# The order of the sixteen row blocks in the last FFN-down sweep of a decoder layer: plain squares and pairs of the seven-product form in turn

## The chip, the cores and the metric

The kernel runs on one core of a Trainium2 chip. The metric is the device time of one execution in microseconds (us). TensorE is called PE, VectorE DVE, ScalarE ACT, GpSimd POOL; SP is the engine whose queue issues the transfers. "L1239" is line 1239 of the kernel before; the change adds one line at 1174, so that every later line stands one number higher in the kernel after.

## The reference

One decoder layer over 256 tokens of width 2048 in float32. Only the last third matters here:

```python
x = x + mix @ w_out
h2 = rms_norm(x, mlp_norm)
x = x + jnp.square(jax.nn.relu(h2 @ w_ffn_up)) @ w_ffn_down      # 2048 -> 8192 -> 2048
gate = jax.nn.sigmoid(rms_norm(x, ple_norm) @ w_ple_gate)
x = x + gate * (p @ w_ple_proj)
out = rms_norm(x, final_norm)
```

`mix` is the output of the mixers that come before (pooling and RWKV-7). The change touches the product with `w_ffn_down` alone.

## The kernel before

**Products in two parts.** Each float32 operand is split into a high part (a copy rounded to PE's format, ACT) and a low part (what the rounding lost, DVE). A product is then three matmuls: high by high, low by high, high by low. Every weight therefore crosses ACT once and DVE once before PE can use it: `wh`, `wl` are high and low of a plain weight block, `w7h`, `w7l` of the blocks that the seven-product form uses as they are, `th`, `tl` of the sums of blocks that it needs.

**The FFN.** The 8192 hidden columns are worked in two halves (`hf` 0 and 1). In each half the up product gives 16 blocks of squared activations of 256 hidden columns each (numbers 0 to 15), and two down sweeps follow, one for each half of the 2048 output columns (`np_`). The tiles of a sweep carry both numbers: `d00`, `d01`, `d11`, `d10` in order of time. `d10` is the last one; it gives output columns 0 to 1023.

**A sweep** (`sweep`, L1311) goes through the 16 blocks in the order of a table (`ORDER[j_]`, `j_` being 0 for the first and 1 for the second sweep of a half). A block is a 2x2 product of squares: 256 hidden columns and 256 tokens on one side, 256 hidden columns and 1024 output columns on the other. Ten blocks (`SEVEN`) are done with seven products of 128x512 tiles instead of eight, 21 matmuls, at the price of sums of weight blocks; the other six (`PLAIN`: 2, 5, 8, 11, 14, 15) are plain squares of 24 matmuls, two splits on DVE and no sums. For six of the ten in the second sweep (0, 3, 4, 7, 10, 12, from `AHEAD`) the sums were made earlier and are read back from memory (`tr`, or two `raw` buffers for the blocks in `BY_RING`); blocks 1, 6, 9, 13 make theirs in the sweep: four extra DVE operations on `raw` (L1293 to L1296).

Within a block of the seven-product form there are four products with sums (`of_sums`: `t1`, `t3`, `t2`, `t4`, high parts first, then low) and three with plain blocks (`of_blocks`). Sums come first after a plain square, blocks first after another block of the seven-product form:

```python
for part in (of_sums, of_blocks) if seq[pos - 1] in PLAIN else (of_blocks, of_sums):
    part()
```

so two neighbours run as sums, blocks, blocks, sums. A third one in a row runs again as blocks, sums.

**Buffers.** `th` and `tl` exist once: the sums of the next block are converted only when PE has read the last ones. Raw weights have a ring of seven buffers, high parts of five, low parts of four, given out in the order of use, so a low part can be written only after the one four places earlier has been read. Eight PSUM banks hold the sweep's results: `p2`, `p3`, `p4`, `d22` (one bank each, fed by both kinds of block) and `p5`, `p7`, `p1`, `p6` (two double banks `w1`, `w2`, fed by the seven-product form alone).

**The end of a sweep.** After the last block of the seven-product form (13 in either order) ACT copies `p1` (L1389), DVE combines `p6`, `p7`, `p5` with it (`u`, L1390 to L1392) and adds the result into the residual stream `xb` for both token halves (two operations of 128x1024, L1411). After the last block of all, the four other banks are added one by one (`residual_` on `p2`, `p3`, `p4`, `d22`, 128x512 each, L1411). In the last sweep the first of these frees the bank into which the next stage's first product goes: `pp`, the projection of the per-layer embeddings (L1475 onward; its first bank is the one of `p2`, its second that of `p3`), whose 48 matmuls alternate with transposes of the new `xb` (`h3t`, L1157) and are followed by the gate product `gt`. The fourth quarter of the gate's weights (`gk`) is split ahead and kept.

**What sets the order.** A scheduler places the instructions of this part by priorities and by its own estimate of when operands are ready: splits, sums and residuals carry high priorities, and each engine then runs its list strictly in order. Three hooks hang on positions in the sweep, not on block numbers: at 12 one half of the residual stream is loaded (`xb` from `xd`, into the slot of block 4's activations), at 13 the other half (into the slot of `tr`), at 15 the embeddings `p` are loaded and split (`ps`).

## Time and profile before

| | us |
|---|---|
| median of 3 runs (lowest, highest) | 1163.5 (1162.97, 1163.73) |
| the profiled execution: its own time | 1163.34 |
| the profiled execution: span from first to last instruction | 1161.6 |
| busy: PE, PE's weight loads, DVE, ACT | 1150.8, 989.2, 920.6, 689.1 |

The time of an execution stands 1.74 us above its span, which begins with the first instruction and ends with the last. A row of the timeline gives the start, the busy time from the first start to the last end of the merged instructions, the engine, the line, the operation, output and inputs, and the count; matmuls overlap in the records, so PE's pace is read from one start to the next. "[x <-Y]" at a row's end is idle time before it and what ended it. SPq is the queue of transfers.

### The profile page before, as it was taken

What the parts mean: (1) busy time and instruction counts of PE and PEld (TensorE: products, weight loads), DVE (VectorE), ACT (ScalarE), POOL (GpSimd) and SP (SyncE); (2) the same over time, 40 slices, a digit from 0 to 9 for tenths busy, and PEclk for the clock granted to TensorE, in tenths of its full rate; (3) what the DMA queues carried; (4) which work ended last, traced back from release to release, by engine and by line L of the source; (5) the groups of instructions that cost most, each with busy time, mean ns of one, the idle gap of its engine ahead of it and who ended that gap; (6) DMA issues with size and microseconds to landing.
All of it is one profiled execution on the core that took longest, in us unless ns stands there. A gap on an engine that the chain in (4) does not pass through costs nothing.

```text
span 1161.6 us, 19313 instructions
## 1 busy us (share of the span) xinstructions
PE 1150.8 (99%) x7348; PEld 989.2 (85%) x7348; DVE 920.6 (79%) x1223; ACT 689.1 (59%) x1220; POOL 17.2 (1%) x77
## 2 busy tenths in 40 slices
PE   9999999999999999999999999999999999999997
PEld 8999998788888888888888888888888888888886
DVE  7886898356676788888989888888878989888843
ACT  5868555667544655555665755555556665669733
POOL 4100000000000000000000000000000000000000
PEclk9999999999999999999999999999999999999999
DMA  7553544453898999985787887998885778996812
GB/s 274 164 171 127 160 151 152 147 165 109 319 328 277 325 342 343 326 327 191 257 291 250 319 298 280 350 332 328 317 302 180 262 266 287 335 327 227 301 36 73
DMA packets 78445, 290.87 MB, mean 250 GB/s; under 512 B 8720, under 2 KB 9744, under 8 KB 74128
## 3 DMA queue, kind: packets, MB, share of 16 engines
q1 hardware_dynamic: 78064, 289.28, 70.8%
q8 instruction: 57, 0.93, 0.3%
q10 hardware_dynamic: 288, 0.37, 0.1%
q14 instruction: 36, 0.29, 0.1%
HBM read 259.20 MB, written 30.41 MB: 249 GB/s over the span
## 4 chain that ended last, share of the span: by engine, by line
PE 96%; DVE 1%; DMA 1%; ACT 1%; issue 0%; DVEq 0%; ACTq 0%; SPq 0%
PE u_w L1135 21%; PE d_p L1239 15%; PE u_w L1140 10%; PE d_w L1239 9%; PE d_d L1239 3%; PE o_b L193 2%; PE o_b L195 2%; PE o_b L194 2%; PE gt_b L193 2%; PE gt_b L195 2%; PE gt_b L194 2%; PE zp_b L193 2%; PE wag_b L380 1%; PE zr_b L184 1%; PE zk_b L184 1%; PE zk_b L185 1%
## 5 line engine op out<-in xcount | busy, mean ns | idle before, releaser
L1135 PE MATMUL u_w<-h,wh_u 128*128 128x512 f32 x1024 | 321.9, 395 | 0.0
L1140 PEld LDWEIGHTS u_w<-h,wl_u 128*128 128x128 f32 x1024 | 192.4, 188 | 45.4
L171 ACT ACTIVATE wh_u<-raw_u 128x512 fp32r<-128x512 f32 x256 | 147.2, 623 | 133.9 <-PE u_w L1135 99.8
L1140 PE MATMUL u_w<-h,wl_u 128*128 128x256 f32 x1024 | 201.4, 278 | 0.0
L172 DVE TENSOR_TENSOR wl_u<-raw_u,wh_u 128x1024 fp32r<-128x1024 f32 x128 | 156.1, 1220 | 38.1 <-PE u_w L1140 22.6
L1135 PEld LDWEIGHTS u_w<-h,wh_u 128*128 128x128 f32 x1024 | 156.1, 189 | 0.1
L1299 ACT ACTIVATE th_d<-raw_d 128x1024 fp32r<-128x1024 f32 x52 | 52.6, 1053 | 63.1 <-DVE raw_d L1295 43.7
L1239 PE MATMUL d_p<-wh_d,yd 128*128 128x512 f32 x288 | 77.0, 389 | 0.0
L1301 DVE TENSOR_TENSOR tl_d<-raw_d,th_d 128x1024 fp32r<-128x1024 f32 x52 | 61.4, 1221 | 12.4 <-ACT th_d L1299 12.3
L172 DVE TENSOR_TENSOR wl_o<-raw_o,wh_o 128x1024 fp32r<-128x1024 f32 x32 | 39.0, 1223 | 31.3 <-ACT wh_o L171 15.9
L1239 PEld LDWEIGHTS d_p<-wh_d,yd 128*128 128x128 f32 x288 | 54.0, 188 | 11.3
L1239 PE MATMUL d_w<-th_d,ys 128*128 128x512 f32 x240 | 61.5, 390 | 0.0
L171 ACT ACTIVATE wh_o<-raw_o 128x512 fp32r<-128x512 f32 x64 | 36.7, 623 | 40.2 <-PE o_b L194 21.7
L171 ACT ACTIVATE wh_d<-raw_d 128x512 fp32r<-128x512 f32 x96 | 53.9, 619 | 7.0 <-DMA raw_d<-in_w_ffn_down_dram 2.7
L172 DVE TENSOR_TENSOR wl_d<-raw_d,wh_d 128x1024 fp32r<-128x1024 f32 x48 | 57.1, 1217 | 0.0
L1288 ACT ACTIVATE w7h_d<-raw_d 128x1024 fp32r<-128x1024 f32 x40 | 42.2, 1056 | 22.1 <-DMA raw_d<-in_w_ffn_down_dram 8.4
L1239 PEld LDWEIGHTS d_w<-th_d,ys 128*128 128x128 f32 x240 | 44.7, 188 | 9.6 <-ACT th_d L1299 0.5
L1290 DVE TENSOR_TENSOR w7l_d<-raw_d,w7h_d 128x1024 fp32r<-128x1024 f32 x40 | 48.8, 1219 | 4.4 <-PE d_d L1239 2.0
L1239 PE MATMUL d_p<-w7h_d,ys 128*128 128x512 f32 x160 | 49.3, 389 | 0.0
L1239 PE MATMUL d_p<-wl_d,yd 128*128 128x512 f32 x144 | 44.3, 389 | 0.0
L1289 ACT ACTIVATE w7h_d<-raw_d 128x512 fp32r<-128x512 f32 x40 | 25.0, 624 | 24.4 <-PE d_d L1239 19.5
L172 DVE TENSOR_TENSOR wl_zp<-raw_zp,wh_zp 128x1024 fp32r<-128x1024 f32 x16 | 19.5, 1223 | 24.6 <-ACT wh_zp L171 24.6
(390 smaller groups left out, 2694.5 us busy)
## 6 DMA issues: line engine op xcount, KB each, us to landing
raw_u<-in_w_ffn_up_dram SPq DMA_DIRECT2D x128, 512.0 KB, 6.3
raw_d<-in_w_ffn_down_dram SPq DMA_DIRECT2D x106, 512.0 KB, 5.9
raw_ta<-in_w_ffn_down_dram SPq DMA_DIRECT2D x44, 512.0 KB, 6.8
tad<-ta SPq DMA_DIRECT2D x22, 1024.0 KB, 5.7
raw_o<-in_w_out_dram SPq DMA_DIRECT2D x32, 512.0 KB, 5.2
tr_d<-tad SPq DMA_DIRECT2D x28, 512.0 KB, 5.1
raw_gt<-in_w_ple_gate_dram SPq DMA_DIRECT2D x24, 512.0 KB, 4.6
raw_zk<-in_w_in_dram SPq DMA_DIRECT2D x16, 512.0 KB, 3.5
```

The costliest lines, as they stand in the source:

```text
L171: nc.scalar.activation(wh[:, a * 512 : (a + 1) * 512], raw[:, a * 512 : (a + 1) * 512], AF.Copy)
L172: nc.vector.tensor_tensor(wl, raw, wh.bitcast(F32), op=ALU.subtract)
L193: nc.tensor.matmul(o, a_h, wh[:, 0:n], start=first, stop=False)
L194: nc.tensor.matmul(o, a_l, wh[:, 0:n], start=False, stop=False)
L195: nc.tensor.matmul(o, a_h, wl[:, 0:n], start=False, stop=last)
L1135: nc.tensor.matmul(bank[:, ct, :].rearrange("p (s t) -> p s t", s=2), wh[:, c], hl, start=k == 0, stop=False, skip_group_check=True,)
L1140: nc.tensor.matmul(bank[:, ct, 0:T], wl[:, c], hl[:, 0, :], start=False, stop=k == 15, skip_group_check=True)
L1239: nc.tensor.matmul(o, l, r, start=first, stop=last, skip_group_check=True)
L1288: nc.scalar.activation(ha, ra, AF.Copy)
L1290: nc.vector.tensor_tensor(la, ra, ha.bitcast(F32), op=ALU.subtract)
L1299: nc.scalar.activation(th[:, r], tr[r], AF.Copy)
L1301: nc.vector.tensor_tensor(tl[:, r], tr[r], th[:, r].bitcast(F32), op=ALU.subtract)
```

## The change

The last sweep gets an order of its own, the other three keep theirs. Seven-product blocks now always stand in pairs, a plain square between each two pairs, and one plain square (15) at the end instead of two (14, 15).

```diff
     ORDER = (tuple(range(16)), (2, 0, 1, 3, 5, 4, 6, 7, 8, 9, 10, 11, 12, 13, 14, 15))
+    LAST = (2, 0, 1, 5, 3, 4, 8, 6, 7, 11, 9, 10, 14, 12, 13, 15)
     SEVEN = tuple(i for i in range(16) if i not in PLAIN)
...
-        seq = ORDER[j_]
+        seq = LAST if hf and j_ else ORDER[j_]
```

No instruction with arithmetic on PE is added or removed; the sweep's matmuls, splits, sums and transfers are the same ones in another order. Up to the fourth block (2, 0, 1) both orders agree. Three places show how the engines' lists moved. In the names `d10_0_13` is the first, `d10_1_13` the second raw tile of block 13 in the sweep `d10`; `ys6` are the activations of block 6.

**PE, between block 6 and block 7.** Before:

```order
L1239 MATMUL d10_p4_9921<-tl_d10_6_10179,ys6_8247 128x512
L1239 MATMUL d10_w2_9924<-w7h0_d10_7_10226,ys7_8355 128x512 x2
L1239 MATMUL d10_w2_9924<-w7l0_d10_7_10228,ys7_8355 128x512
L1239 MATMUL d10_p2_9919<-w7h1_d10_7_10227,ys7_8355 128x512 x2
L1239 MATMUL d10_p2_9919<-w7l1_d10_7_10229,ys7_8355 128x512
L1239 MATMUL d10_p3_9920<-w7h0_d10_7_10226,ys7_8355 128x512 x2
L1239 MATMUL d10_p3_9920<-w7l0_d10_7_10228,ys7_8355 128x512
L1239 MATMUL d10_w1_9923<-th_d10_7_10224,ys7_8355 128x512 x4
```

After:

```order
L1240 MATMUL d10_p4_9921<-tl_d10_6_10217,ys6_8247 128x512
L1240 MATMUL d10_w2_9924<-w7h0_d10_6_10218,ys6_8247 128x512 x2
L1240 MATMUL d10_w2_9924<-w7l0_d10_6_10220,ys6_8247 128x512
L1240 MATMUL d10_p2_9919<-w7h1_d10_6_10219,ys6_8247 128x512 x2
L1240 MATMUL d10_p2_9919<-w7l1_d10_6_10221,ys6_8247 128x512
L1240 MATMUL d10_p3_9920<-w7h0_d10_6_10218,ys6_8247 128x512 x2
L1240 MATMUL d10_p3_9920<-w7l0_d10_6_10220,ys6_8247 128x512
L1240 MATMUL d10_w2_9924<-w7h0_d10_7_10264,ys7_8355 128x512 x2
```

Before, 6 and 7 followed block 4, 6 began with its blocks, and 7 therefore had only its own nine block matmuls between the sums of 6 and its own sums. After, 6 follows the plain square 8 and begins with its sums, and the blocks of 6 and of 7 lie between the two groups of sums.

**DVE, from the low parts of block 13 to the residual additions.** Before, from the second low part of block 14:

```order
L172 TENSOR_TENSOR wl_d10_1_14_10527<-raw_d10_1_14_10519,wh_d10_1_14_10526 128x1024
L177 TENSOR_TENSOR ps_10561<-raw_pT_10559,ps_10561 128x512
L172 TENSOR_TENSOR wl_d10_0_15_10565<-raw_d10_0_15_10555,wh_d10_0_15_10564 128x1024
L1390 TENSOR_TENSOR u_d10_10510<-d10_w2_9924,u_d10_10510 128x512
L172 TENSOR_TENSOR wl_d10_1_15_10570<-raw_d10_1_15_10557,wh_d10_1_15_10569 128x1024
L1391 TENSOR_TENSOR u_d10_10510<-d10_w1_9923,u_d10_10510 128x512
L1392 TENSOR_TENSOR u_d10_10510<-u_d10_10510,d10_w1_9923 128x2x512
L1411 SCALAR_TENSOR_TENSOR xb4_10469<-u_d10_10510,s2sq_4333,xb4_10469 128x1024 x2
L1411 SCALAR_TENSOR_TENSOR xb4_10469<-d10_p2_9919,s2sq_4333,xb4_10469 128x512
L172 TENSOR_TENSOR wl_pp0_0_10610<-raw_pp0_0_10607,wh_pp0_0_10609 128x1024
L1411 SCALAR_TENSOR_TENSOR xb4_10469<-d10_p3_9920,s2sq_4333,xb4_10469 128x512
```

After, from the low parts of 13's sums:

```order
L1302 TENSOR_TENSOR tl_d10_13_10510<-raw_d10_0_13_10505,th_d10_13_10509 128x1024
L1302 TENSOR_TENSOR tl_d10_13_10510<-raw_d10_1_13_10507,th_d10_13_10509 128x1024
L172 TENSOR_TENSOR wl_d10_0_15_10565<-raw_d10_0_15_10555,wh_d10_0_15_10564 128x1024
L172 TENSOR_TENSOR wl_d10_1_15_10570<-raw_d10_1_15_10557,wh_d10_1_15_10569 128x1024
L172 TENSOR_TENSOR wl_pp0_0_10610<-raw_pp0_0_10607,wh_pp0_0_10609 128x1024
L1391 TENSOR_TENSOR u_d10_10548<-d10_w2_9924,u_d10_10548 128x512
L172 TENSOR_TENSOR wl_pp1_0_10650<-raw_pp1_0_10647,wh_pp1_0_10649 128x1024
L1392 TENSOR_TENSOR u_d10_10548<-d10_w1_9923,u_d10_10548 128x512
L1393 TENSOR_TENSOR u_d10_10548<-u_d10_10548,d10_w1_9923 128x2x512
L177 TENSOR_TENSOR gk01_10809<-raw_gk0_10806,gk00_10808 128x512
L1412 SCALAR_TENSOR_TENSOR xb4_10464<-u_d10_10548,s2sq_4333,xb4_10464 128x1024 x2
L1412 SCALAR_TENSOR_TENSOR xb4_10464<-d10_p2_9919,s2sq_4333,xb4_10464 128x512
```

Before, the four low parts of 14 and 15 come after 13's sums, and the combination `u` and the residuals are run while PE works on 14 and 15. After, only 15 is left behind 13; between 13's sums and the residual of `p2` there now also stand the low parts of the first two tiles of the projection (`wl_pp0`, `wl_pp1`) and one of the kept gate weights (`gk01`), which all stood behind the residual of `p2` before.

**SP's queue, the transfers around the end of the sweep.** Before (the second tile of 13 and the load of `xb4` stand right ahead of the first row):

```order
L163 DMA raw_d10_0_14_10517<-in_w_ffn_down_dram 128x1024
L163 DMA raw_d10_1_14_10519<-in_w_ffn_down_dram 128x1024
L163 DMA raw_d10_0_15_10555<-in_w_ffn_down_dram 128x1024
L163 DMA raw_d10_1_15_10557<-in_w_ffn_down_dram 128x1024
L163 DMA raw_pT_10559<-in_pT_dram 128x512
L1482 DMA fn_10765<-in_final_norm_dram 128x2048
L163 DMA raw_pp0_0_10607<-in_w_ple_proj_dram 128x1024
L163 DMA raw_pp1_0_10647<-in_w_ple_proj_dram 128x1024
L163 DMA raw_pp2_0_10687<-in_w_ple_proj_dram 128x1024
L163 DMA raw_pp3_0_10727<-in_w_ple_proj_dram 128x1024
L163 DMA raw_gt0_0_10787<-in_w_ple_gate_dram 128x1024
L163 DMA raw_gk0_10806<-in_w_ple_gate_dram 128x1024
```

After:

```order
L1483 DMA fn_10765<-in_final_norm_dram 128x2048
L1420 DMA xb4_10464<-xd3_6935 128x2048
L163 DMA raw_d10_1_13_10507<-in_w_ffn_down_dram 128x1024
L163 DMA raw_d10_0_15_10555<-in_w_ffn_down_dram 128x1024
L163 DMA raw_d10_1_15_10557<-in_w_ffn_down_dram 128x1024
L163 DMA raw_pT_10559<-in_pT_dram 128x512
L163 DMA raw_pp0_0_10607<-in_w_ple_proj_dram 128x1024
L163 DMA raw_pp1_0_10647<-in_w_ple_proj_dram 128x1024
L163 DMA raw_gt0_0_10787<-in_w_ple_gate_dram 128x1024
L163 DMA raw_pp2_0_10687<-in_w_ple_proj_dram 128x1024
L163 DMA raw_pp3_0_10727<-in_w_ple_proj_dram 128x1024
L163 DMA raw_gk0_10806<-in_w_ple_gate_dram 128x1024
```

The final norm's weights (`fn`, 1 MB) and `xb4` (1 MB) have moved ahead of the second tile of block 13, and `gt0_0` ahead of the last two tiles of the projection. The load of `gk0` keeps its place behind these.

## The prediction

> **What bounds the kernel now.** I read the page first: busy time and the chain of waits.

> ```profile
> PE 1150.8 (99%) x7348; PEld 989.2 (85%) x7348; DVE 920.6 (79%) x1223; ACT 689.1 (59%) x1220; POOL 17.2 (1%) x77
> PE 96%; DVE 1%; DMA 1%; ACT 1%; issue 0%; DVEq 0%; ACTq 0%; SPq 0%
> ```

> PE is the bound, and the chain that ended last runs on it for 96% of the span. So the change can gain only where PE stands, and loses wherever it makes PE stand. Next the list of PE's waits (line waited for: us in all, times, longest us), and the stages from the last sweep on (stretch: length, then busy us of PE, weight loads, DVE, ACT, POOL; granted clock, DMA share, GB/s):

> ```profile
> PE warm_b L349 <- DVE ones L107: 1.2, 1, 1.2
> PE h2t L1157 <- DVE h L1164: 0.4, 1, 0.4
> PE zp_b L195 <- DVE wl_zp L172: 0.3, 1, 0.3
> 969.90:1050.50 80.60, 80.60 (x355) 66.28 (x354) 72.88 (x79) 48.80 (x69) 0.00 (x0) 1.00 0.90 324
> 1050.50:1064.20 13.70, 13.70 (x74) 11.21 (x72) 12.15 (x18) 13.70 (x32) 0.00 (x0) 1.00 0.87 290
> 1064.20:1153.60 89.40, 88.98 (x443) 75.23 (x440) 53.58 (x76) 49.47 (x97) 0.00 (x0) 1.00 0.41 138
> ```

> None of the 1.9 us of waits lies in a down sweep. The sweep is the first stretch: PE full, DVE 72.88 of 80.60 (90%), so DVE has little slack behind PE. In the next, the projection `pp`, ACT is full as well as PE. Then PE is dense until the gate product ends; I see nothing there that would give back a delay.

> **The change, part by part.** *What can be gained.* Matmuls are the same, so the gain is at most the sweep's idle time. By starts, nine block matmuls take 2.04 us, twelve sum matmuls 2.72 (1036.93 to 1039.65 below), a plain square 5.44 (1039.65 to 1045.09): six plains and ten blocks of 4.76 are 80.24, against 969.93 to 1050.53 = 80.60. Nearly all of the missing 0.36 is at block 7, the third in a row:

> ```profile
> 1004.59 1.99 ACT L1299 ACTIVATE th_d<-tr_d 128x1024 fp32r<-128x1024 f32 x2
> 1006.50 2.35 DVE L1301 TENSOR_TENSOR tl_d<-tr_d,th_d 128x1024 fp32r<-128x1024 f32 x2
> 1006.64 1.66 PE L1239 MATMUL d_w<-th_d,ys 128*128 128x512 f32 x6
> 1009.70 1.09 PE L1239 MATMUL d_p<-wh_d,yd 128*128 128x512 f32 x4
> ```

> Its sums take 1006.64 to 1009.70 = 3.06 instead of 2.72: `th` is ready only at 1006.58 and `tl` at 1008.85, because both wait for the sums of 6, nine matmuls earlier. With pairs, eighteen block matmuls (4.08 us) lie between, and between pairs a plain square. I take the whole 0.34 as gained (between 0 and 0.36).

> *What is moved: the end of the sweep.* The next stage's first product needs the bank of `p2`, so it waits for the residual of `p2` on DVE. The path of before, on PE, ACT and DVE:

> ```profile
> 1030.13 1.52 PE L1239 MATMUL d_w<-th_d,ys 128*128 128x512 f32 x6
> 1036.93 1.52 PE L1239 MATMUL d_w<-th_d,ys 128*128 128x512 f32 x6
> 1039.65 1.07 PE L1239 MATMUL d_p<-wh_d,yd 128*128 128x512 f32 x4
> 1045.09 1.07 PE L1239 MATMUL d_p<-wh_d,yd 128*128 128x512 f32 x4
> 1050.53 0.39 PE L193 MATMUL pp_b<-wh_pp,ps 128*128 128x512 f32 x1
> 1029.43 0.63 ACT L1289 ACTIVATE w7h_d<-raw_d 128x512 fp32r<-128x512 f32 x1 [1.58 <-PE d_d L1239]
> 1030.16 0.69 DVE L1291 TENSOR_TENSOR w7l_d<-raw_d,w7h_d 128x512 fp32r<-128x512 f32 x1 [0.88 <-ACT w7h_d L1289]
> 1034.20 0.69 DVE L1296 TENSOR_TENSOR raw_d<-raw_d,raw_d 128x512 f32<-128x512 f32 x1
> 1034.82 1.22 DVE L172 TENSOR_TENSOR wl_d<-raw_d,wh_d 128x1024 fp32r<-128x1024 f32 x1
> 1035.95 2.35 DVE L1301 TENSOR_TENSOR tl_d<-raw_d,th_d 128x1024 fp32r<-128x1024 f32 x2
> 1038.22 1.22 DVE L172 TENSOR_TENSOR wl_d<-raw_d,wh_d 128x1024 fp32r<-128x1024 f32 x1
> 1039.36 0.68 DVE L177 TENSOR_TENSOR ps<-raw_pT,ps 128x512 fp32r<-128x512 f32 x1
> 1039.96 1.22 DVE L172 TENSOR_TENSOR wl_d<-raw_d,wh_d 128x1024 fp32r<-128x1024 f32 x1
> 1041.10 0.68 DVE L1390 TENSOR_TENSOR u_d<-d_w,u_d 128x512 f32<-128x512 f32 x1
> 1041.70 1.21 DVE L172 TENSOR_TENSOR wl_d<-raw_d,wh_d 128x1024 fp32r<-128x1024 f32 x1
> 1042.83 0.68 DVE L1391 TENSOR_TENSOR u_d<-d_w,u_d 128x512 f32<-128x512 f32 x1
> 1043.55 1.22 DVE L1392 TENSOR_TENSOR u_d<-u_d,d_w 128x1024 f32<-128x1024 f32 x1
> 1044.80 2.48 DVE L1411 SCALAR_TENSOR_TENSOR xb<-u_d,s2sq,xb 128x1024 f32<-128x1024 f32 x2
> 1047.20 0.75 DVE L1411 SCALAR_TENSOR_TENSOR xb<-d_p,s2sq,xb 128x512 f32<-128x512 f32 x1
> 1047.86 1.22 DVE L172 TENSOR_TENSOR wl_pp<-raw_pp,wh_pp 128x1024 fp32r<-128x1024 f32 x1
> ```

> Plain 11 ends at 1030.13. Block 13's low parts begin 0.03 later: they and its high parts go into the buffers that plain 11's last products free (the ACT row waits for `d_d`, the bank of those products). From there DVE runs without a gap to the residual of `p2`, done at 1047.86: 17.70 us, while PE needs 1050.53 - 1030.13 = 20.40 (12, 13, 14, 15). DVE is 2.67 ahead.

> After, 13 is again the second block behind a plain square, now 14, and the low parts' ring puts its first low part four places behind a tile of 14, as it was behind one of 11. So the chain again starts at a plain's end, but PE has only 12, 13, 15 left: 4.76 x 2 + 5.44 = 14.96. DVE's list loses the two low parts of 14 (2 x 1.13) and gains two of the projection (2 x 1.13) and one of the kept gate weights. By differences of starts: 13's low parts and four sums 1030.16 to 1034.82 = 4.66; `ps` 0.60; `tl` of 13 2.27; 15's low parts and the projection's two, four at 1.13 = 4.52; `u` 0.60 + 0.72 + 1.25; the gate weight 0.60 (shape and operation of `ps`); wide residual 2.40; residual of `p2` 0.66. Sum 18.28.

> Ahead of 12 PE now does what it did before and one plain more: plain 14 ends at 1030.13 + 5.44 - 0.34 = 1035.23. DVE starts at 1035.26 and is done at 1053.54; PE is done with 15 at 1035.23 + 14.96 = 1050.19 and stands 3.35. The projection starts at 1053.54 instead of 1050.53: **+3.01**, the 0.34 included.

> Ahead of that, 13's sums on PE start at 1042.03. `tl` of 13 is done at 1035.26 + 7.53 + 0.08 = 1042.87; its low matmuls begin at 1042.03 + 1.81 = 1043.84. Cover 0.97; if gone, PE slips, but DVE's end, not PE's, sets the stage, so I cost it at nothing. On ACT the first conversion of 15 and `ps` now stand ahead of 13's `th`, and DVE's `tl` waits for `th`. 15's first tile is issued after 14's low parts, by about 1027.6, and lands 7.8 later at 1035.4; ACT is through with both by about 1037.5, while 13's sums are there from 1039.3 on: nothing, cover 1.8. ACT's copy for `u` starts at 1044.75, when 13 ends; DVE comes to `u` 10.92 into the chain, at 1046.2: nothing, cover 0.8.

> *The gate weight's transfer.* It stands before both residuals on DVE, and everything behind it waits.

> ```profile
> 1041.21 0.33 SPq L163 DMA_DIRECT2D raw_gk<-in_w_ple_gate_dram  x1
> DMA to landing us min/median/max: 5.1/5.3/6.9
> 1048.08 1.15 ACT L176 ACTIVATE gk<-raw_gk 128x512 fp32r<-128x512 f32 x2 [1.50 <-DMA raw_gk<-in_w_ple_gate_dram]
> raw_d<-in_w_ffn_down_dram SPq DMA_DIRECT2D x8, 512.0 KB, 7.8
> ```

> Before, ACT waited for this very transfer, off the path. After, it is issued when 15's first low part frees the raw buffer: 8.66 into the chain, 1043.92. Landing after 5.1, 5.3 or 6.9 us and half of ACT's 1.15 give 1049.6, 1049.8 or 1051.4; DVE comes to it 14.62 into the chain, at 1049.88. Extra 0, 0 or 1.5: I take **+0.2**, near the median.

> *The other moved transfers.* 13's second tile now follows `fn` and `xb4` (1 MB each) on SP. I place its issue at about 1026.5 (14's first low part, after 10's `tl`): with 7.8 us for a weight tile it lands at 1034.3, and ACT needs it by about 1035.3. Zero, cover 1.0; each us beyond it moves the whole chain. The first tiles of the projection land long before DVE reaches them.

> *The next stage.* It is ACT-full, and ACT's list now has the second kept gate weight's two halves (1.15) and the sums of squares of both token halves ahead of the first copies out of `pp`:

> ```profile
> 1051.97 1.05 ACT L296 ACTIVATE junk_n<-xb 128x1024 f32<-128x1024 f32 x1
> ```

> While PE stands, ACT can do conversions that it did in the stage before, so the stage may give back up to 0.7 (by starts, 48 matmuls at 0.227 and six transposes at 0.35 are 13.0 of 13.7); or its copies come 1.15 later plus a landing, up to 1.4 lost. I take **+0.4**, the middle: neither end has a nearer row.

> Sum, against the profiled execution's own 1163.34 (0.16 below the median of 1163.5): 1163.34 + 3.01 + 0.2 + 0.4 = 1166.95, or 1167.0.

> *The clock.* A gap of 3.35 us is the longest that PE would have. The end of the trace shows how long the clock holds:

> ```profile
> 1152.90 0.28 PE L1528 MATMUL gt3c<-gk,h 128*128 128x256 f32 x1
> 1153.00:1156.00 3.00, 0.18 (x2) 0.00 (x0) 1.84 (x6) 2.46 (x5) 0.00 (x0) 1.00 0.00 0
> 1156.00:1159.00 3.00, 0.00 (x0) 0.00 (x0) 0.94 (x3) 0.78 (x2) 0.00 (x0) 0.71 0.63 236
> ```

> The mean of 0.71 from 1156 on puts the fall to half clock at 1157.26, 4.1 us after the last matmul's end at 1153.18. By that row 3.35 keeps the clock. [...]

> **The rivals.**

> B, *a transfer decides*: gate weight or 13's second tile at the slow end. For it: 13's tile behind 2 MB; landings spread by 1.8 us. Against: medians just suffice. 1.0 to 2.5 more: 1168.0 to 1169.5.

> C, *the gap trips the clock*: by the row's own reaction time, 4.1 us at half clock, 2.05 lost: 1163.34 + 3.01 + 0.2 + 0.4 + 2.05 = 1169.0. Against: 3.35 is less than 4.1. It decides from about 0.7 more of gap.

> D, *the stage gives back*: no loss in `pp` but 0.7 regained or more, with the gate weight on time: 1163.34 + 3.01 - 0.7 = 1165.7, down to 1165.0 if ACT's work done ahead spares also the stage's later copies.

> E, *not slower*: DVE isn't late, because 13's low parts find a free buffer before plain 14 ends. It decides at a start 3.35 earlier, by 1031.9. Then PE has no gap: 1163.34 - 0.34 = 1163.0. For it: DVE has idle time in the sweep (10%). Against: the 1030.16 row, in the same place of the ring.

> **How the numbers follow.** My forecast 0.57, with its own range 1166.2 to 1167.9; B 0.18; C 0.07; D 0.11; E 0.05; 0.02 for a gain that no row shows. A measurement can tell 0.2%, 2.3 us, from no change, so slower begins at 1165.8: forecast, B and C are slower, 0.82 less 0.01 of the forecast's low tail, 0.81; D and E are the same, 0.17 with that tail; faster 0.02. The range from 1165.2 to 1169.5 leaves out E, the unseen gain, part of D and the ends of B and C.

> **What the profile after would show.** Block 7's sums 2.72 from start to start, where 3.06 stood. On DVE no gap from 14's end to the residual of `p2`, 18.3 us long. On PE one wait of about 3.4 ahead of the projection's first matmul, put down to DVE's `xb`, at a clock of 1.00. At the gate weight's low part no wait over 0.2 for ACT's `gk`; more means B. The projection's stage 13.7 to 14.5 long, the gate product as before. The forecast is wrong if 13's low parts start away from 14's end, if that wait is split over several lines, or if the stages after shrink by as much as PE waited.

## The result and the profile after

| | before | after |
|---|---|---|
| median of 5 runs (lowest, highest), us | 1163.5 (1162.97, 1163.73) | 1168.56 (1166.58, 1169.25) |
| ratio, with its 95% interval | | 1.0041 [1.003, 1.0053] |
| the profiled execution: its own time, span, us | 1163.34, 1161.6 | 1169.13, 1167.4 |

The kernel became slower by 5 us, 1.6 us above the predicted time. That lies inside the stated range (1165.2 to 1169.5), but above the forecast's own range (1166.2 to 1167.9): it is covered because the stated range also takes in two rivals, B and C. Unlike before, the runs after lie up to 2.7 us apart. The page and the list of PE's waits of the profile after:

```profile
PE 1152.2 (99%) x7348; PEld 990.7 (85%) x7348; DVE 920.5 (79%) x1223; ACT 689.8 (59%) x1220; POOL 18.2 (2%) x77
PE 93%; DVE 3%; DMA 2%; ACT 1%; issue 1%; SPq 0%; DVEq 0%; ACTq 0%
PE pp_b L193 <- DVE xb L1412: 3.7, 1, 3.7
```

A wait that was not there before now leads the list: PE stands 3.7 us at the projection's first matmul, for DVE's residual. The timeline of PE around it, with the sums of block 7 above and the last matmul of the program below:

```profile
1012.06 1.52 PE L1240 MATMUL d_w<-th_d,ys 128*128 128x512 f32 x6
1014.78 1.07 PE L1240 MATMUL d_p<-wh_d,yd 128*128 128x512 f32 x4
1049.69 0.61 PE L1240 MATMUL d_d<-wl_d,yd 128*128 128x512 f32 x2
1054.01 0.77 PE L193 MATMUL pp_b<-wh_pp,ps 128*128 128x512 f32 x1 [3.70 <-DVE xb L1412]
1059.22 0.60 PE L1157 MATMUL h3t<-ident,xb 128*128 128x128 f32 x4
1158.71 0.28 PE L1529 MATMUL gt3c<-gk,h 128*128 128x256 f32 x1
```

Three things are to be seen. The sums of 7 take 1012.06 to 1014.78 = 2.72 us, where they took 3.06. The projection begins at 1054.01, 3.48 later than before. And its twelve matmuls take 1054.01 to 1059.22 = 5.21 us, where they took 2.73 (before, the transposes behind them start at 1053.26). The path on DVE, and two rows of ACT that it waits for:

```profile
1035.15 1.22 DVE L1291 TENSOR_TENSOR w7l_d<-raw_d,w7h_d 128x1024 fp32r<-128x1024 f32 x1 [1.29 <-PE d_d L1240]
1050.11 0.69 DVE L177 TENSOR_TENSOR gk<-raw_gk,gk 128x512 fp32r<-128x512 f32 x1 [0.23 <-ACT gk L176]
1053.11 2.06 DVE L1412 SCALAR_TENSOR_TENSOR xb<-d_p,s2sq,xb 128x512 f32<-128x512 f32 x3
1035.76 0.63 ACT L1290 ACTIVATE w7h_d<-raw_d 128x512 fp32r<-128x512 f32 x1 [3.34 <-DMA raw_d<-in_w_ffn_down_dram]
1049.45 1.15 ACT L176 ACTIVATE gk<-raw_gk 128x512 fp32r<-128x512 f32 x2 [1.87 <-DMA raw_gk<-in_w_ple_gate_dram]
```

DVE begins 13's low parts when plain 14's products (`d_d`) end, and runs from there to the residuals with one listed wait of 0.23 for the gate weight. The granted clock of PE (the third number from the end of a row; the first numbers are the stretch, its length and PE's busy time) explains the slow matmuls:

```profile
1048.92:1052.33 3.41, 1.38 (x7) 0.80 (x5) 3.17 (x4) 2.88 (x6) 0.00 (x0) 1.00 0.83 335
1052.33:1055.75 3.42, 1.75 (x4) 1.49 (x5) 3.42 (x5) 2.64 (x5) 0.00 (x0) 0.50 0.01 6
1055.75:1059.16 3.41, 3.41 (x9) 2.54 (x9) 2.35 (x3) 1.25 (x4) 0.00 (x0) 0.50 0.30 79
1059.16:1062.57 3.41, 3.41 (x19) 2.80 (x18) 1.83 (x2) 3.41 (x8) 0.00 (x0) 1.00 0.81 275
```

It fell to half at 1052.33, in the gap, and came back at 1059.16: 6.83 us, twice 3.41.

### The profile page after: what moved, and what is told of

Read it like the earlier page. It is cut to its first block, busy times and chain, and to the rows that moved or that the text cites. A ratio compares the mean times of both kernels' runs of the same rounds, so it can differ in the third digit from the quotient of the medians.

```text
span 1167.4 us, 19316 instructions
## 1 busy us (share of the span) xinstructions
PE 1152.2 (99%) x7348; PEld 990.7 (85%) x7348; DVE 920.5 (79%) x1223; ACT 689.8 (59%) x1220; POOL 18.2 (2%) x77
## 4 chain that ended last, share of the span: by engine, by line
PE 93%; DVE 3%; DMA 2%; ACT 1%; issue 1%; SPq 0%; DVEq 0%; ACTq 0%
PE u_w L1135 20%; PE d_p L1240 14%; PE u_w L1140 10%; PE d_w L1240 9%; PE d_d L1240 3%; PE o_b L193 2%; PE o_b L194 2%; PE o_b L195 2%; PE gt_b L195 2%; PE gt_b L194 2%; PE gt_b L193 2%; PE zp_b L193 1%; PE zr_b L184 1%; PE zk_b L184 1%; PE zr_b L185 1%; PE zk_b L185 1%
## 5 line engine op out<-in xcount | busy, mean ns | idle before, releaser
L172 DVE TENSOR_TENSOR wl_u<-raw_u,wh_u 128x1024 fp32r<-128x1024 f32 x128 | 156.1, 1221 | 37.8 <-PE u_w L1140 21.0
L172 DVE TENSOR_TENSOR wl_o<-raw_o,wh_o 128x1024 fp32r<-128x1024 f32 x32 | 39.0, 1223 | 31.9 <-ACT wh_o L171 16.3
L172 DVE TENSOR_TENSOR wl_d<-raw_d,wh_d 128x1024 fp32r<-128x1024 f32 x48 | 56.9, 1218 | 0.0
L1289 ACT ACTIVATE w7h_d<-raw_d 128x1024 fp32r<-128x1024 f32 x40 | 42.2, 1055 | 21.1 <-DMA raw_d<-in_w_ffn_down_dram 12.9
L1291 DVE TENSOR_TENSOR w7l_d<-raw_d,w7h_d 128x1024 fp32r<-128x1024 f32 x40 | 48.8, 1220 | 5.3 <-ACT w7h_d L1290 2.3
L1302 DVE TENSOR_TENSOR tl_d<-tr_d,th_d 128x1024 fp32r<-128x1024 f32 x28 | 33.0, 1221 | 8.4 <-ACT th_d L1300 8.4
## 6 DMA issues: line engine op xcount, KB each, us to landing
raw_u<-in_w_ffn_up_dram SPq DMA_DIRECT2D x128, 512.0 KB, 6.0
raw_d<-in_w_ffn_down_dram SPq DMA_DIRECT2D x106, 512.0 KB, 5.9
raw_ta<-in_w_ffn_down_dram SPq DMA_DIRECT2D x44, 512.0 KB, 6.5
raw_o<-in_w_out_dram SPq DMA_DIRECT2D x32, 512.0 KB, 5.2
tr_d<-tad SPq DMA_DIRECT2D x28, 512.0 KB, 5.5
raw_gt<-in_w_ple_gate_dram SPq DMA_DIRECT2D x24, 512.0 KB, 4.7
raw_zk<-in_w_in_dram SPq DMA_DIRECT2D x16, 512.0 KB, 3.5
```

The costliest lines, as they stand in the source:

```text
L172: nc.vector.tensor_tensor(wl, raw, wh.bitcast(F32), op=ALU.subtract)
L1289: nc.scalar.activation(ha, ra, AF.Copy)
L1291: nc.vector.tensor_tensor(la, ra, ha.bitcast(F32), op=ALU.subtract)
L1302: nc.vector.tensor_tensor(tl[:, r], tr[r], th[:, r].bitcast(F32), op=ALU.subtract)
```

## The experiments

**One plain square at the end, the rest as before.** The order up to block 11 is that of before, triples included.

```diff
-    LAST = (2, 0, 1, 5, 3, 4, 8, 6, 7, 11, 9, 10, 14, 12, 13, 15)
+    LAST = (2, 0, 1, 3, 5, 4, 6, 7, 8, 9, 10, 11, 14, 12, 13, 15)
```

> The last sweep keeps before's order up to block 11 (triples included) and ends 14, 12, 13, 15: only the end is changed. Here five splits of later weights stand between 13's sums and the residual of p2 on DVE, two more than after. Theory: plain 14 ends 5.44 after 1030.13, DVE's list from there is 18.28 + 1.13 + 0.60 = 20.0, PE's 14.96: PE stands 5.1 us, so 1163.34 + 5.1 = 1168.4, and with a gap of that length the clock falls to half in every run, for some 2.5 more: 1170 to 1171.5. Rival (the clock's fall in the profile of after has nothing to do with the gap): 1168.4 with a clock of 1.00 in some runs. Rival (the loss comes from the pairs): 1163 to 1164.

Measured: 1170.34 us (1170.13 to 1171.2), ratio 1.006 [1.0047, 1.0072]. PE's wait and two stretches of the clock:

```profile
PE pp_b L193 <- DVE xb L1412: 4.5, 1, 4.5
1050.89:1054.30 3.41, 0.00 (x0) 0.00 (x0) 3.41 (x4) 1.92 (x4) 0.00 (x0) 0.99 0.88 309
1054.30:1057.71 3.41, 2.87 (x7) 2.29 (x8) 3.41 (x5) 2.14 (x4) 0.00 (x0) 0.51 0.16 55
```

The end alone makes the kernel slower, and by more than the whole change: with two more splits ahead of the residual, PE's wait is 0.8 longer. The mean clock was 0.994 to 0.996 in all five runs, where before has 0.997 or 0.998. The wait was 0.6 shorter than reckoned. In this profile 9.4 us lie between the start of the last matmul and the end, against 8.7 in the nine others; why, stays open.

**Pairs throughout, two plain squares at the end.**

```diff
-    LAST = (2, 0, 1, 5, 3, 4, 8, 6, 7, 11, 9, 10, 14, 12, 13, 15)
+    LAST = tuple(range(16))
```

> The last sweep runs 0, 1, 2, ... 15: pairs of the seven-product form throughout, as after, but two plain squares (14, 15) at the end, as before. Theory (the loss comes from the single plain square at the end, which leaves DVE's list 3.3 to 3.7 us behind PE; the pairs themselves are free): no wait ahead of the projection, the sums of 7 take 2.72 us, 1163.0 us, within 0.2% of before, and the runs lie within 1 us of one another. Rival (the loss comes from the pairs' order, by its transfers or its conversions in the sweep): PE stands in the sweep and the time stays 2 us or more above before, 1165.5 to 1168.5.

Measured: 1165.42 us (1164.61 to 1166.24, 11 runs), ratio 1.0017 [1.0009, 1.0026]. A miss: PE stands in the sweep, as the rival has it, and the time lies 0.1 below the rival's range. The waits, and their two rows on PE's timeline:

```profile
PE d_w L1240 <- ACT th_d L1300: 1.7, 2, 1.2
981.39 0.74 PE L1240 MATMUL d_w<-th_d,ys 128*128 128x512 f32 x2 [0.49 <-ACT th_d L1300]
1002.41 1.66 PE L1240 MATMUL d_w<-th_d,ys 128*128 128x512 f32 x6 [1.17 <-ACT th_d L1300]
```

There is no wait ahead of the projection, and the sums of 7 take 2.72 here too (PE's starts at 1009.37 and 1012.09); so much of the theory holds. But this order starts with block 0 instead of plain square 2, and PE now stands at the sums of 3 and of 6 for ACT's `th`. So the pairs alone are not free in every order; the run tells nothing against them in the order of the change, whose profile lists no wait in the sweep. Why the conversion of `th` is late here was not followed up.

**Two splits behind the residual.** The order of after; the low parts of the projection's second tile and of the kept gate weight may issue on DVE only behind the residual of `p2`.

```diff
+            with tc.issue_after(first_res[0]) if name in ("pp1_0",) else nullcontext():
                 nc.vector.tensor_tensor(wl, raw, wh.bitcast(F32), op=ALU.subtract)
...
+            with tc.issue_after(first_res[0]) if kp == 0 else nullcontext():
                 split_sb(wh, wl, raw[:, a * 512 : (a + 1) * 512])
```

> The order of after, but the low parts of the projection's second tile and of the kept gate weight may issue on DVE only behind the residual of p2. Nothing else is changed. Theory: DVE's list is 1.13 + 0.60 shorter and loses the 0.23 wait for the gate weight: PE's wait falls from 3.70 to about 1.75; 1163.34 + 3.48 - 1.95 = 1164.9, and with so short a gap the clock stays at full speed, so the runs lie within 1 us: 1164.4 to 1165.4. Rival (a transfer or the bank's last matmul sets the start, not DVE's list): the wait stays near 3.7 and the time at 1166.5 to 1169.

Measured: 1164.99 us (1164.26 to 1168.02, 11 runs), ratio 1.0016 [1.0007, 1.0025].

```profile
1052.09 0.47 PE L194 MATMUL pp_b<-wh_pp,ps 128*128 128x512 f32 x1 [1.64 <-DVE xb L1414]
1154.41 0.28 PE L1533 MATMUL gt3c<-gk,h 128*128 128x256 f32 x1
```

1.73 us less on DVE and no wait for the gate weight, 2.06 less of PE's wait: DVE's list sets the start. The spread was not as expected: one of eleven runs took 1168.02 at a mean clock of 0.996; it has no trace, so what happened in it stays open.

**Matmuls in the gap.** After the last block, ahead of the projection:

```diff
     ph, pl = ps_
+    junk = wide_bank("junk")
+    for _ in range(13):
+        nc.tensor.matmul(junk[:, 0], ph[:, 0:128], ph[:, 0:512], start=True, stop=True)
```

> The kernel after, with 13 additional matmuls of 128x512 on PE between the last one of block 15 and the first of the projection (2.95 us of work into a bank that is free there, never read). Nothing waits for them that would not wait anyway. Theory (2 to 2.7 us of after's loss are a clock at half speed that the gap sets off): the clock stays at 1.00, the projection begins at the same time, and the time falls to 1166.4 to 1166.9 in every run, with a spread under 1 us. Rival (the slow matmuls in the profile of after are set off by something else, the transfers or the projection itself): same as after, 1166.6 to 1169.3, with the same spread.

Measured: 1166.37 us (1165.93 to 1168.09, 7 runs), ratio 1.0026 [1.0016, 1.0037], the mean clock 0.998 or 0.999 in all seven.

```profile
1051.20 3.11 PE L1475 MATMUL junk<-ps 128*128 128x512 f32 x13
1055.33 0.50 PE L193 MATMUL pp_b<-wh_pp,ps 128*128 128x512 f32 x1 [1.02 <-DVE xb L1412]
1157.67 0.28 PE L1532 MATMUL gt3c<-gk,h 128*128 128x256 f32 x1
```

3 us of useless work on PE make the kernel 2 us faster than after: no run's mean clock lies below those of before, and in the profile the clock is 1.00 throughout the projection. The projection doesn't start sooner: the gap itself is still lost. The spread is wider than expected. In this profile (the run of 1168.09) it isn't the clock: the whole sweep began 0.9 us later than in after's, and DVE stood 0.60 for the conversion of 13's second tile. The other runs have no trace.

**The kernel after again,** beside the three that follow.

> The kernel after once more, as the measure for the runs beside it. Theory: PE waits 3.5 to 3.8 us ahead of the projection in each run (DVE's list); the clock falls to half in most runs but not in all, as where its periods lie differs from run to run. A run without the fall takes 1166.4 to 1166.9, one with it 1168 to 1169.3, the mean granted clock 0.998 and 0.995 to 0.996.

Measured: 1168.88 us (1166.24 to 1170.12, 5 runs), ratio 1.0044 [1.003, 1.0059]. By run, time and mean clock: 1166.24 at 0.998, 1167.27 at 0.997, 1168.88 at 0.994, 1169.14 and 1170.12 at 0.995. In the profile of the second:

```profile
PE pp_b L193 <- DVE xb L1412: 3.1, 1, 3.1
1049.51:1052.92 3.41, 0.32 (x2) 0.00 (x0) 3.41 (x5) 2.47 (x5) 0.00 (x0) 1.00 0.53 215
1052.92:1056.33 3.41, 3.37 (x8) 2.73 (x9) 3.41 (x5) 2.92 (x6) 0.00 (x0) 0.50 0.02 5
```

PE's wait was 3.1 here: the gate weight came in time, and 13's second tile too. The clock fell as PE resumed and stayed down for 3.41 us instead of 6.83. An estimate of its price is half of the work done in it, 3.37 / 2 = 1.7 us; from the projection's first matmul to the program's last this profile takes 1052.96 to 1156.85 = 103.89 us, 1.52 more than before.

**The gate weight alone behind the residual.** The second half of the edit of two splits.

> The order of after, but the low part of the kept gate weight alone may issue on DVE only behind the residual of p2. Theory for the start: DVE's list is 0.60 shorter and loses the 0.23 wait for the gate weight's conversion, so PE waits 2.87 instead of 3.70: 1165.7 to 1166.1 without a fall of the clock. Theory for the clock: in the profiles so far the clock fell after a period of 3.41 us in which PE had stood 2.1, and not where it had stood 0.6 or 1.6; so about 2 us of standing in one period suffice, a gap of 2.87 still puts that much into one period in about two of three runs, and these take 1167.4 to 1168.6 at a mean clock of 0.995 to 0.997. [...]

Measured: 1167.38 us (1166.13 to 1168.1, 5 runs), ratio 1.0033 [1.002, 1.0046]; mean clock 0.996 or 0.997.

```profile
PE pp_b L193 <- DVE xb L1415: 3.1, 1, 3.1
1036.39 0.69 DVE L1293 TENSOR_TENSOR w7l_d<-raw_d,w7h_d 128x512 fp32r<-128x512 f32 x1 [0.30 <-ACT w7h_d L1291]
1047.68:1051.10 3.42, 2.37 (x11) 1.63 (x9) 3.35 (x4) 1.09 (x3) 0.00 (x0) 1.00 0.99 375
1051.10:1054.51 3.41, 1.31 (x6) 1.13 (x7) 3.41 (x6) 2.91 (x6) 0.00 (x0) 1.00 0.42 169
1054.51:1057.92 3.41, 3.41 (x11) 2.63 (x10) 3.08 (x4) 2.38 (x6) 0.00 (x0) 0.50 0.18 32
```

The clock fell at 1054.51, 1.3 us after PE had resumed work, at the end of a period in which PE had worked 1.31 of 3.41 us. So the fall came here without a whole period of standing: the gap was 3.15 us, and the two periods ahead of the fall have 2.37 and 1.31 us of work. Four of the five runs lie at 1167.33 to 1168.1, one at 1166.13. The wait was 0.28 longer than reckoned, which is 13's second tile: its conversion came 0.30 late.

**The projection in another bank.**

```diff
-f"pp{n}", copy_out))
+f"pp{n}", copy_out, banks=None if n else (lambda b: [b[:, 0], b[:, 1]])(wide_bank("pp0w"))))
```

> The order of after, but the projection's first product goes into the double bank that u's operands leave free, instead of the banks of p2 and p3. DVE's list is the same. Theory (the wait is for the bank, through DVE's residual of p2): no wait ahead of the projection, which begins at 1050.15; its twelve matmuls end at 1052.87, and the transposes behind them wait for the residual of p2 until about 1053.95, 1.1 us; the clock stays at full speed. 1163.34 - 0.38 + 1.1 = 1164.1, between 1163.6 and 1165.0. Rival (another operand of the projection sets its start: its low weights or ps): the wait ahead of its first matmul stays near 3.7 and the time at 1166.5 or more.

Measured: 1163.78 us (1163.48 to 1164.56, 11 runs), ratio 1.0004 [0.9995, 1.0013]. No wait ahead of the projection; one is left at the transposes:

```profile
1054.38 0.33 PE L1157 MATMUL h3t<-ident,xb 128*128 128x128 f32 x1 [0.79 <-DVE xb L1412]
```

With the order of DVE's list up to the residuals unchanged, the bank alone takes the loss away: it was the bank of `p2`, not weights or `ps`, that PE waited for.

**Residuals first.** The order of after; residuals of `p2` and `p3` ahead of the wide ones, later splits behind these.

```diff
-                    for tt in range(2):
-                        residual_(n0, tt, u[...], 1024)
+                    def wide_res(): ...
+                    if seq is not LAST:
+                        wide_res()
...
                     if end:
                         residual_((n0, n1)[b], tt, o)
+                        if seq is LAST and which == "p3":
+                            wide_res()
...
+            with tc.issue_after(first_res[0]) if name in ("pp1_0", "pp2_0") else nullcontext():
```

> The order of after with DVE's list at the end changed: the residuals of p2 and p3 ahead of the two wide ones, and the low parts of the projection's second and third tile and of the kept gate weight only behind these. Theory: the residual of p2 is done at about 1047.5 and that of p3 at 1049, ahead of PE (1050.15); the wide ones at 1052.4, when PE needs them at 1052.9; p4's at 1054.2, when PE needs it at 1054.2. PE stands less than 0.3 us in all, so the time is 1163.0 to 1163.5, the same as before: then all of the loss was the order on DVE, and what the pairs gain, 0.34 us, is too little to be measured. Rival (transfers or ACT in the projection's stage hold it back as well): 1164.5 or more.

Measured: 1163.25 us (1162.76 to 1164.13, 11 runs), before beside it 1163.49 (20 runs); ratio 0.9998 [0.9989, 1.0007].

```profile
PE pp_b L194 <- ACT pp L1488: 0.3, 1, 0.3
1049.49 0.39 PE L194 MATMUL pp_b<-wh_pp,ps 128*128 128x512 f32 x1
1046.36 0.74 DVE L1420 SCALAR_TENSOR_TENSOR xb<-d_p,s2sq,xb 128x512 f32<-128x512 f32 x1
1047.62 0.74 DVE L1420 SCALAR_TENSOR_TENSOR xb<-d_p,s2sq,xb 128x512 f32<-128x512 f32 x1
```

The two small residuals are done at 1047.1 and 1048.4, ahead of the projection's start at 1049.49. The whole loss was the order on DVE's list. What the pairs gain doesn't show above what a measurement can tell, so no version measured here beats before clearly.

## Why the prediction was right, and which term it missed

The mechanism that the forecast is built on happened: DVE's list made PE stand ahead of the projection. The size was off by 1.6 us, mainly because the clock fell, which the forecast did not count on. That the median still lies in the stated range is in part luck: the forecast's own range misses it, and rival C (1169.0), given 0.07, comes nearer.

**The gain in the sweep: right.** 3.06 became 2.72 at block 7, 0.34 as forecast.

**DVE's list: right.** It began at 1035.15 (forecast 1035.26) with plain 14's end, and the residual of `p2` began at 1053.11 (forecast 1053.54 - 0.66 = 1052.88). From the one to the other it took 17.96 instead of 17.62: 0.23 at the gate weight, which the forecast has as a term of its own of 0.2, and 0.13 at the second low part of 13, which it doesn't have and which the earlier start nearly makes up. The projection started 3.48 later instead of 3.21, for the most part because I ended the list with the step of 0.66 to the next DVE row, but PE is released by the end of the operation, which takes 0.75, and begins 0.15 after it (1053.11 + 0.75 = 1053.86, 1054.01).

**13's second tile: cover thinner than said.** I put it at 1.0 us. ACT waited for that transfer until 1035.76 in the profile after, which cost 0.13; DVE stood 0.30 for it in the run with the gate weight alone and 0.60 in the run with matmuls in the gap. It did not decide (rival B), but can add to the spread.

**The projection's stage: the term of 0.4 was mis-sized, it is nothing.** From the projection's first matmul to the program's last: 1050.53 to 1152.90 = 102.37 us before; with the gap but without a fall of the clock 1052.09 to 1154.41 = 102.32 (two splits behind) and 1055.33 to 1157.67 = 102.34 (matmuls in the gap). Neither of the two effects that I set against each other, ACT's work done ahead and its later copies, shows in it; whether they cancel, no run tells.

**The clock: the step that failed.** In the profile after the same stretch is 1054.01 to 1158.71 = 104.70, 2.33 more, and 3.48 + 2.33 = 5.81 is the difference of the two profiled executions (1169.13 - 1163.34 = 5.79). I gave this 0.07 as rival C, with 2.05 us, since "by that row 3.35 keeps the clock". The row was misread. I took the 4.1 us at the end of the program for a delay that starts with the last matmul. The changes of the clock lie whole periods of 3.413 us apart, across PE's work and its gaps: in the profile after at 1052.33, 1059.16 and 1161.56, 2 and 30 periods apart, in that of after again at 1052.92 and 1162.14, 32 apart. I read this as periods that go on whatever PE does, with the clock of the next one following from how much PE worked in the one before. The end of before read in such periods:

```profile
1150.44:1153.85 3.41, 2.74 (x23) 2.53 (x22) 0.63 (x4) 1.07 (x4) 0.00 (x0) 1.00 0.17 65
1153.85:1157.26 3.41, 0.00 (x0) 0.00 (x0) 2.72 (x8) 2.69 (x5) 0.00 (x0) 1.00 0.06 21
```

The last matmul fell into a period that was busy for 2.74 us; the clock fell at the end of the next. The 4.1 is a period and what was left of the one before. Nor did a fall need 0.7 more of gap, as C has it: PE stood 3.70 in the profile after, 0.35 more than forecast, and the clock also fell at waits of 3.13 (after again) and 3.15 (the gate weight alone). The matmuls in the gap show that the fall belongs to the gap: with them no run's mean clock is below 0.998, and the median fell by 2.2 us to 1166.37, inside what the forecast gave for a clock that holds (1166.2 to 1167.9). The two runs of after at 0.998 lie there too (1166.58 and 1166.24); that the clock held in them is read from the mean alone, as they have no trace.

Rival D, the stage giving time back, and rival E, no delay, did not happen: the stage is unchanged, and DVE's list began at plain 14's end.

## What to carry to other kernels

Before work is moved ahead of a stage's end, list what the engine behind the bound still has to do from its last fixed point (here a ring of buffers that a plain square frees) to the bank that the next stage needs, and compare it with what the bound engine has left. A step that gains 0.3 us on PE can take away 5.4 us of cover on DVE. A priority list fills an engine's idle places with later work that is ready, and that work then stands ahead of the short operation for which everything waits; to let the few releasing operations issue first was worth more here than the order of the blocks.

## What the hardware showed unexpectedly

```profile
1048.56:1051.97 3.41, 1.88 (x9) 1.23 (x7) 3.38 (x5) 3.03 (x6) 0.00 (x0) 1.00 0.59 241
1051.97:1055.38 3.41, 3.29 (x17) 2.76 (x18) 3.41 (x5) 2.86 (x6) 0.00 (x0) 1.00 0.02 5
1155.32:1158.73 3.41, 1.81 (x16) 1.60 (x14) 1.14 (x4) 1.49 (x2) 0.00 (x0) 1.00 0.01 2
1158.73:1162.14 3.41, 0.00 (x0) 0.00 (x0) 1.86 (x6) 1.76 (x5) 0.00 (x0) 1.00 0.32 118
1162.14:1165.55 3.41, 0.00 (x0) 0.00 (x0) 0.00 (x0) 0.00 (x0) 0.00 (x0) 0.50 0.53 190
```

So in these traces standing for about 60% of a period (1.38 us of work) was enough for the fall, and standing for about 47% (1.81) was not. Where the limit lies between, no run shows. At half speed the clock came back after periods with 3.41 (after, the gate weight alone), 3.37 (after again) and 2.87 us of work (one plain square at the end), and not after one with 1.75 (after).

In the traces a gap of 3.1 to 4.5 us thus cost its own time and one period at half speed (gaps of 3.13, 3.15 and 4.5) or two (3.70). The gap's length alone does not order them; where the periods lay against the gap may, which is my reading of four traces. The two runs of after at a mean clock of 0.998 may have had none; they have no trace. The runs of after spread in keeping with this: by and large the slower ones have the lower mean clocks (1166.24 us at 0.998, 1167.27 at 0.997, 1169.14 at 0.995).
